# Softmax by a min-reduction, output gates of two pairs together, first gate of the delta rule earlier, 32 products from GpSimd to VectorE

## The chip, the cores and the metric

The kernel runs on one core of a Trainium2 chip. The time is device microseconds of that core; each kernel is run several times and the median counts. TensorE (PE in the profile, PEld for its weight loads) multiplies matrices into PSUM; VectorE (DVE), ScalarE (ACT) and GpSimd (POOL) do everything elementwise; SyncE (SP) issues the DMAs.

## The reference, cut to what matters

The program is a small network on 512 positions of width 1024, all in float32. A first block has two layers of feed-forward, mixer, feed-forward; the mixer of its second layer is a sparse attention ("dsa"). A second block has a gated delta rule ("gdn") and a forgetting attention ("fox"). The change touches these three:

```
# dsa: 8 heads of 128; the keys that are not among the top 256 are masked
s = einsum(q, k_sel) * 128 ** -0.5 ;  p = softmax(where(valid, s, -inf)) ;  o = p @ v

# gdn: 16 value heads, chunks of 128 positions in the kernel
q_dec = q * exp(g)                      # decayed queries
o = q_dec @ state + attn @ v_new        # a scan over the chunks
o = rmsnorm(o, norm_w) * silu(z)        # z: the gate, a projection of the input

# fox: 16 heads of 64
q = rmsnorm(q) * 64 ** -0.5 ; k = rmsnorm(k)          # x * root, per head
logits = q @ k + cum[t] - cum[s], masked causally ; p = softmax(logits) ; o = (p @ v) * silu(z)
```

## The kernel before

Every float32 product is done as three fast matmuls on split operands (a high and a low part: `xh`, `xl` for data, `wh`, `wl` for weights; lines 145 to 147). A weight tile of 128 x 1024 is loaded by SP (`raw`, line 138), cast by ACT to `wh` (139) and subtracted to `wl` by DVE (140); three tiles of each kind rotate. A projection of 128 outputs over the 512 positions is 8 x 3 = 24 matmuls of 512 columns into one PSUM bank of the tag "acc", of which there are three; the bank is free again when its last reader is through.

The kernel is written as one stream of calls. A planner, at build time, draws up the order of each engine's queue: of the instructions that it reckons ready it takes the one that stands first in the stream (`tc.high_priority()` lifts some). So work that stands later fills holes in earlier work, as far as buffers allow, and where a call stands in the stream is its rank. On the chip each engine keeps the drawn-up order and waits where an input is late.

**gdn** (line 967) goes through 8 groups of two value heads. `stage_a(gi)` projects a query and a key tile, convolves them on DVE (1022), normalises them, makes the matrices `Am` and `At` (1121 to 1123), the decayed queries `qd` (1127, on GpSimd, two products of 128 x 512 per group) and the inverse of a triangular system: its small blocks in a chain on DVE (1144, 1146), then DMAs and small matmuls (1169 to 1207). `stage_v` projects and convolves the values, `stage_z` the gate (two projections, a tanh on ACT at 1015 and a product on DVE at 1016, into `zg`, one buffer), `stage_b` is the scan over four chunks, `stage_g` the norm with the gate, `stage_o` the output projection. They are called in the order a(0), a(1), v(0), then for each group v(gi+1), a(gi+2), b(gi), z(gi), g(gi), o(gi-1). `self.late()` (1632) scales the eight tiles of the residual.

**fox** (line 1351) goes through 8 pairs of heads. For pair p there are eight score steps (two heads x four query blocks): `scores` (1466) makes the logits, one DVE instruction adds `ncb` and takes the row maximum (1475), DVE negates it (1477), ACT takes the exponential with its sum (1478), DVE the reciprocal (1479) and the product (1480); `turn` transposes the block (1489, 1490) one step later; `values` (1493) multiplies with v and the gate `zs`. Between these steps, written out by hand, `fill.run` puts in the projections of the next pair, in units of three matmuls: q, k, then for an even pair v, for an odd pair the gates of both pairs (`z_done`, 1432). `normed` squares q or k out of PSUM, makes the root `r` seven units later (173 to 177) and multiplies `x` by it on GpSimd (1403); q and k are then split into halves (1415 to 1425). Exponential and logarithm share one table of ACT, which `self.log_exp()` loads; Silu needs another.

**dsa** (line 784) has the same softmax with the scale as a factor: 895 reduces, 897 multiplies by -DSA_SCALE, 898 exponentiates, 900 multiplies on ACT; 32 steps in all. Beside them runs the top-k of line 881, 882 on DVE.

Of the kernel before, what the change touches and what calls it, by code (L numbers as in the profile page):

```python
# [12 lines left out]
AF = mybir.ActivationFunctionType  # L13
ALU = mybir.AluOpType
# [14 lines left out]
def f32(ap):  # L29
    return ap.bitcast(F32)  # L30
# [410 lines left out]
def c4(ap, c):  # L441
    return ap[:, c * P:(c + 1) * P]
# [275 lines left out]
DSA_SCALE = 128.0 ** -0.5  # L718
TAKEN = -3.0e38
# [64 lines left out]
def dsa(self, tables):  # L784
    nc, tc, A = self.nc, self.tc, self.A
    with tc.tile_pool(name="ds", bufs=1) as ds:
        def T(name, shape=(P, S), dtype=F32, bufs=None):
            return ds.tile(list(shape), dtype, name=name, bufs=bufs)
# [26 lines left out]
        ps = self.bank()  # L815
# [39 lines left out]
        bias = [cneg]  # L855
        for i in range(1, 4):
            W = (i + 1) * P
            x = T(f"isc{i}", (P, W))

            for t in range(2):  # L860
# [3 lines left out]
                for a, ps in enumerate(pair):  # L864
                    hh = 2 * t + a
                    r = self.tmp()
# [22 lines left out]
        def scores(h, i):  # L889
            W = (i + 1) * P  # L890
            ps = self.bank("sa")
            nc.tensor.matmul(ps[:, :W], c4(qT[h], i), kT[h // 4][:, :W], start=True, stop=True)
            x = T("p", bufs=3)[:, :W]
            st = T("st", (P, 4), bufs=4)
            nc.vector.tensor_tensor_reduce(x, ps[:, :W], bias[i], 1.0, TAKEN, op0=ALU.add, op1=ALU.max,
                                           accum_out=st[:, 0:1])
            nc.vector.tensor_scalar(st[:, 1:2], st[:, 0:1], -DSA_SCALE, None, op0=ALU.mult)
            nc.scalar.activation(x, x, AF.Exp, scale=DSA_SCALE, bias=st[:, 1:2], accum_out=st[:, 2:3])
            nc.vector.reciprocal(st[:, 3:4], st[:, 2:3])
            nc.scalar.activation(x, x, AF.Copy, scale=st[:, 3:4])  # L900
            prob[h, i] = x
# [65 lines left out]
def gdn(self, feed0, gate, tail):  # L967
    nc, tc, A = self.nc, self.tc, self.A
    with tc.tile_pool(name="gd", bufs=1) as gd, tc.tile_pool(name="gdd", bufs=1, space=bass.MemoryType.DRAM) as dr:
        def T(name, shape=(P, S), dtype=F32, bufs=None):  # L970
            return gd.tile(list(shape), dtype, name=name, bufs=bufs)
# [10 lines left out]
        ps, ps_q, ps_k = [self.bank() for _ in range(3)]  # L982
# [31 lines left out]
        def silu2(out, x, t):  # L1014
            nc.scalar.activation(t, x, AF.Tanh, scale=0.5)
            nc.vector.scalar_tensor_tensor(out, t, 1.0, x, op0=ALU.add, op1=ALU.mult)
# [55 lines left out]
        def wtile(m):  # L1072
            return self.weights(A["a_in"][m], 1024)

        def stage_a(gi):
# [3 lines left out]
            for u in range(2):  # L1079
                if gi == 0:  # L1080
                    ps = (ps_q, ps_k)[u]
                else:
                    ps = self.bank()
                    self.project(ps, wtile(u * 8 + gi), 0, self.xh, self.xl)
                x = T(f"x{u}", bufs=2 + u)
# [3 lines left out]
            rb, r, pk = norms(qk, 1.0, "sa", gi < 2)  # L1089
# [5 lines left out]
            q, k = qk  # L1095
            kkm, qkm = T("gt", bufs=2), T("gt", bufs=2)
            for src, dst, mi in ((k, kkm, 0), (q, qkm, 1)):
                ps = self.aux()
# [5 lines left out]
            gbc = T("big", (P, 2, S), bufs=3)  # L1104
# [9 lines left out]
            for a in range(2):  # L1114
                e = self.tmp()
                for c in range(4):
                    nc.scalar.activation(c4(e, c), gbc[:, a, c * P:(c + 1) * P], AF.Relu, scale=-1.0,
                                         bias=gcol[:, c, hs[a]:hs[a] + 1])
# [5 lines left out]
            nc.scalar.activation(gbc, gbc, AF.Exp, bias=ln_qs)  # L1124
            qd = T("qd", (P, 2, S), bufs=2)
            for a in range(2):
                nc.gpsimd.tensor_mul(qd[:, a], q, gbc[:, a])

# [35 lines left out]
            for n in range(8):  # L1166
                for q in quart:
                    r = slice(q.start, q.start + 16)
# [42 lines left out]
        def stage_v(gi):  # L1211
            hs = (2 * gi, 2 * gi + 1)
            vn = T("vnat", (P, 4, 2, P), bufs=2)
            for a in range(2):
                ps = self.bank()
                self.project(ps, wtile(16 + hs[a]), 0, self.xh, self.xl)
                x = T("cv", bufs=2)
                conv(ps, 16 + hs[a], x)
                pv = self.bank("sb")
                for c in range(4):  # L1220
                    nc.tensor.transpose(c4(pv, c), c4(x, c), self.ident)
                nc.scalar.activation(vn[:, :, a, :], pv.rearrange("p (c d) -> p c d", c=4), AF.Copy, scale=0.5)
            return vn

        def stage_z(gi):
            zg = T("zg", (P, 2, S))
            for a in range(2):
                ps = self.bank()
                self.project(ps, wtile(32 + 2 * gi + a), 0, self.xh, self.xl)
                silu2(zg[:, a], ps, zg[:, a])  # L1230
            return zg
# [65 lines left out]
        def stage_o(gi, og):  # L1297
            for m4 in range(2):
                wo = self.weights(A["a_out"][gi, m4], 1024)
                for u in range(4):  # L1300
                    m = 4 * m4 + u
                    ps = self.bank()
                    self.project(ps, wo, u * 256, [o[0] for o in og], [o[1] for o in og])
                    with tc.high_priority():
                        nc.vector.scalar_tensor_tensor(self.h[m], ps, gate[:, m:m + 1], self.h[m], op0=ALU.mult,
                                                       op1=ALU.add)

        og, last = {}, []
        st = {gi: stage_a(gi) for gi in range(2)}
        vs = {0: stage_v(0)}  # L1310
        for gi in range(8):
            if gi < 7:
                vs[gi + 1] = stage_v(gi + 1)
            if gi < 6:
                st[gi + 2] = stage_a(gi + 2)
            if gi == 0:
                self.late()
            oT = stage_b(gi, st.pop(gi), vs.pop(gi))
            z = stage_z(gi)
            og[gi] = stage_g(gi, oT, z)  # L1320
            if gi:
                stage_o(gi - 1, og.pop(gi - 1))
# [28 lines left out]
def fox(self, feed, gate, tail):  # L1351
    nc, tc, A = self.nc, self.tc, self.A
    BF = dt.bfloat16
    with tc.tile_pool(name="fx", bufs=1) as fx, tc.tile_pool(name="fxd", bufs=1, space=bass.MemoryType.DRAM) as dr:
        def T(name, shape=(P, S), dtype=F32, bufs=None):
            return fx.tile(list(shape), dtype, name=name, bufs=bufs)
# [13 lines left out]
        ps, ps_q, ps_k = [self.bank() for _ in range(3)]  # L1370
        self.project_halves([(ps, next(feed), 16, 16), (ps_q, next(feed), P, P), (ps_k, next(feed), P, P)])
        fb = self.prm("b_f_bias")[:16]
        e, z, one = self.tmp()[:16], self.tmp()[:16], self.tmp()[:16]
# [13 lines left out]
        qs, ks, vs, zs, og = {}, {}, {}, {}, []  # L1387

        def normed(name, dst, p, gain_col, sq_scale, eps, halves):
            def done(ps):  # L1390
                x, sq, sh = T("x", bufs=2), self.tmp(), T("sqh", dtype=F32R, bufs=2)
                nc.scalar.activation(sq, ps, AF.Square, scale=sq_scale)
                nc.scalar.activation(x, ps, AF.Copy, scale=gain_col)
                nc.scalar.activation(sh, ps, AF.Square, scale=sq_scale)
                sl = T("sql", dtype=F32R, bufs=2)
                nc.vector.tensor_sub(sl, sq, f32(sh))

                def stats():
                    pn = self.bank()
                    nc.tensor.matmul(pn, blk, sh, start=True, stop=False)  # L1400
                    nc.tensor.matmul(pn, blk, sl, start=False, stop=True)
                    r = self.rstd_from(pn, T("r", bufs=2), eps)
                    nc.gpsimd.tensor_mul(x, x, r)  # L1403
                    dst[p] = halves(x)
                fill.later(7, stats)
            return done
# [21 lines left out]
        def v_copy(p):  # L1428
            v = vs[p] = vs[p + 1] = T("v", (P, 4, 256), bufs=2)
            return lambda c2, ps: nc.scalar.copy(v[:, 2 * c2:2 * c2 + 2].rearrange("p c d -> p (c d)"), ps)  # L1430

        def z_done(p):
            def done(ps):
                zs[p] = T("sz", bufs=2)
                nc.scalar.activation(zs[p], ps, AF.Silu)
                self.log_exp()
            return done

        def q_done(p):
# [24 lines left out]
        nbs, prob, pTs = {}, {}, {}  # L1464

        def scores(p, a, i):
            q, (k, kl) = qs[p][:, a], ks[p]
            W = (i + 1) * P
            ps = self.bank("sa")
            nc.tensor.matmul(ps[:, :W], c4(q, i), k[:, a, :W], start=True, stop=False)  # L1470
            nc.tensor.matmul(ps[:, :W], c4(q, i), kl[:, a, :W], start=False, stop=False)
            nc.tensor.matmul(c4(ps, i), ib, mb, start=False, stop=True)
            x = T("p", bufs=3)[:, :W]
            st = T("st", (P, 4), bufs=4)
            nc.vector.tensor_tensor_reduce(x, ps[:, :W], nbs[p][:, a, :W], 1.0, TAKEN, op0=ALU.add, op1=ALU.max,  # L1475
                                           accum_out=st[:, 0:1])
            nc.vector.tensor_scalar(st[:, 1:2], st[:, 0:1], -1.0, None, op0=ALU.mult)
            nc.scalar.activation(x, x, AF.Exp, bias=st[:, 1:2], accum_out=st[:, 2:3])  # L1478
            nc.vector.reciprocal(st[:, 3:4], st[:, 2:3])
            nc.vector.tensor_scalar(x, x, st[:, 3:4], None, op0=ALU.mult)  # L1480
            prob[p, a, i] = x
# [28 lines left out]
        for t in range(len(steps) + 2):  # L1510
            if t < len(steps):
                p, a, i = steps[t]
# [246 lines left out]
```

## Time and profile before

| | |
|---|---|
| runs of the kernel before | 2765.12, 2759.53, 2767.68 us; median 2765.12 |
| the profiled execution | 2762.07 us, its span 2760.3 us, granted clock 0.99 |
| busy, of the span | PE 2674.5 us (97%), PEld 2186.6 (79%), DVE 1719.7 (62%), ACT 1211.2 (44%), POOL 197.4 (7%) |
| stages on the time axis | dsa from about 1280 to 1460 us, gdn from about 1840 to 2400, fox from about 2400 to the end |

PE's busy time is that of pipelined matmuls, one after another without a hole in most of the span; the time that a change can win is where PE waits or runs at the lower clock.

### The profile page before, as it was taken

What the parts mean: (1) busy time and instruction counts of PE and PEld (TensorE: products, weight loads), DVE (VectorE), ACT (ScalarE), POOL (GpSimd) and SP (SyncE); (2) the same over time, 40 slices, a digit from 0 to 9 for tenths busy, and PEclk for the clock granted to TensorE, in tenths of its full rate; (3) what the DMA queues carried; (4) which work ended last, traced back from release to release, by engine and by line L of the source; (5) the groups of instructions that cost most, each with busy time, mean ns of one, the idle gap of its engine ahead of it and who ended that gap; (6) DMA issues with size and microseconds to landing.
All of it is one profiled execution on the core that took longest, in us unless ns stands there. A gap on an engine that the chain in (4) does not pass through costs nothing. (4 is left out here: it accounts for less than half of the span.)

```text
span 2760.3 us, 38266 instructions
## 1 busy us (share of the span) xinstructions
PE 2674.5 (97%) x14903; PEld 2186.6 (79%) x14903; DVE 1719.7 (62%) x3081; ACT 1211.2 (44%) x2248; POOL 197.4 (7%) x184
## 2 busy tenths in 40 slices
PE   8999999999999999999899999999899999999998
PEld 6888878788888888887678888887778777777776
DVE  6454567764545744446966434468788777687776
ACT  4222244532223422223265222246655555577774
POOL 0000002000000000002420000011100000110101
PEclk9999999999999999999999999999999999999999
DMA  5343432244434433333212333223333343132221
GB/s 180 119 138 114 128 97 70 76 140 120 138 114 117 130 112 103 93 94 88 76 39 78 98 99 95 93 76 108 85 115 102 101 113 97 53 101 71 79 65 64
DMA packets 106708, 274.59 MB, mean 99 GB/s; under 512 B 35464, under 2 KB 39552, under 8 KB 106528
## 3 DMA queue, kind: packets, MB, share of 16 engines
q1 hardware_dynamic: 106528, 272.15, 32.6%
q8 instruction: 118, 1.93, 0.3%
q14 instruction: 62, 0.51, 0.1%
HBM read 267.79 MB, written 4.31 MB: 99 GB/s over the span
## 5 line engine op out<-in xcount | busy, mean ns | idle before, releaser
L145 PE MATMUL acc<-xh,wh 128*128 128x512 f32 (+2 forms) x2320 | 909.9, 393 | 21.1 <-ACT xh L186 8.7
L139 ACT CAST wh<-raw 128x1024 fp32r<-128x1024 f32 (+3 forms) x430 | 439.3, 1022 | 1070.0 <-PE acc L146 706.8
L146 PE MATMUL acc<-xl,wh 128*128 128x512 f32 (+1 forms) x2320 | 903.5, 390 | 3.3 <-POOL xl L151 2.4
L147 PE MATMUL acc<-xh,wl 128*128 128x512 f32 (+1 forms) x2320 | 897.8, 387 | 1.8 <-DVE wl L140 1.8
L140 DVE TENSOR_TENSOR wl<-raw,wh 128x1024 fp32r<-128x1024 f32 (+2 forms) x410 | 489.9, 1196 | 80.9 <-ACT wh L139 76.9
L145 PEld LDWEIGHTS acc<-xh,wh 128*128 128x128 f32 (+1 forms) x2320 | 435.9, 188 | 111.8 <-issue 9.1
L146 PEld LDWEIGHTS acc<-xl,wh 128*128 128x128 f32 x2320 | 435.7, 188 | 91.9 <-POOL xl L151 3.9
L147 PEld LDWEIGHTS acc<-xh,wl 128*128 128x128 f32 x2320 | 435.0, 188 | 91.0 <-DVE wl L140 3.2
L146 PE MATMUL acc<-al,wh 128*128 128x512 f32 (+1 forms) x720 | 278.2, 386 | 0.0
L147 PE MATMUL acc<-ah,wl 128*128 128x512 f32 (+1 forms) x720 | 277.7, 386 | 0.0
L145 PE MATMUL acc<-ah,wh 128*128 128x512 f32 (+1 forms) x720 | 277.4, 386 | 0.0
L249 DVE SCALAR_TENSOR_TENSOR h<-acc,h 128x512 f32<-128x512 f32 x128 | 88.4, 690 | 215.8 <-PE acc L147 215.3
L289 DVE TENSOR_TENSOR tmp<-acc,rstd 128x512 f32<-128x512 f32 x88 | 60.9, 691 | 240.3 <-PE acc L147 240.3
L287 DVE TENSOR_TENSOR tmp<-acc,rstd 128x512 f32<-128x512 f32 x88 | 60.8, 691 | 176.7 <-PE acc L147 176.6
L146 PEld LDWEIGHTS acc<-al,wh 128*128 128x128 f32 x720 | 135.2, 188 | 28.7 <-DVE al L151 0.8
L145 PEld LDWEIGHTS acc<-ah,wh 128*128 128x128 f32 x720 | 135.2, 188 | 28.1
L147 PEld LDWEIGHTS acc<-ah,wl 128*128 128x128 f32 x720 | 135.2, 188 | 28.1
L140 POOL TENSOR_TENSOR wl<-raw,wh 128x1024 fp32r<-128x1024 f32 (+1 forms) x20 | 47.8, 2392 | 872.3 <-ACT wh L139 861.2
L145 PE MATMUL acc<-ogh,wh 128*128 128x512 f32 (+1 forms) x256 | 104.0, 408 | 2.4 <-DVE h L310 2.0
L147 PE MATMUL acc<-ogh,wl 128*128 128x512 f32 (+1 forms) x256 | 99.0, 387 | 0.0
L146 PE MATMUL acc<-ogl,wh 128*128 128x512 f32 (+1 forms) x256 | 98.9, 387 | 0.0
L150 ACT CAST ah<-tmp 128x512 fp32r<-128x512 f32 x88 | 54.9, 623 | 63.4 <-DVE tmp L290 63.4
(450 smaller groups left out, 3438.3 us busy)
## 6 DMA issues: line engine op xcount, KB each, us to landing
raw<-in_wi_dram SPq DMA_DIRECT2D x176, 512.0 KB, 3.7
raw<-in_wo_dram SPq DMA_DIRECT2D x64, 512.0 KB, 3.4
raw<-in_ada_w_dram SPq DMA_DIRECT2D x48, 512.0 KB, 3.6
raw<-in_a_in_dram SPq DMA_DIRECT2D x48, 512.0 KB, 3.9
raw<-in_b_in_dram SPq DMA_DIRECT2D x24, 512.0 KB, 3.6
raw<-in_wo_dram SPq DMA_DIRECT2D x24, 384.0 KB, 3.1
raw<-in_a_out_dram SPq DMA_DIRECT2D x16, 512.0 KB, 4.0
big<-rd SPq DMA_DIRECT2D x13, 512.0 KB, 4.9
```

What stands on the lines that cost most here:

```text
L139: nc.scalar.copy(wh[:, :n], raw[:, :n])
L140: self.lo_eng.tensor_tensor(wl[:, :n], raw[:, :n], f32(wh[:, :n]), op=ALU.subtract)
L145: nc.tensor.matmul(out, ah, bh, start=start, stop=False)
L146: nc.tensor.matmul(out, ah, bl, start=False, stop=False)
L147: nc.tensor.matmul(out, al, bh, start=False, stop=stop)
L150: self.nc.scalar.copy(hi, x)
L249: nc.vector.scalar_tensor_tensor(self.h[m], ps, scale(m), self.h[m], op0=ALU.mult, op1=ALU.add)
L287: nc.vector.tensor_mul(t, pg, rstd)
L289: nc.vector.tensor_mul(u, pu, rstd)
```

## The change

In both softmaxes the reduction works on the negated logits and takes their minimum, so that its result is the negated maximum already; the negation goes, and the exponential is taken with scale -1. In gdn the decayed queries, and in fox the products with the root, go from GpSimd to VectorE. In gdn the gate of group 0 is called between a(0) and a(1). In fox the gate of an even pair stays in its PSUM bank until that of the odd pair is there too, and both Silu follow each other, with one reload of the exponential's table behind them.

```diff
@@ dsa scores
-            nc.vector.tensor_tensor_reduce(x, ps[:, :W], bias[i], 1.0, TAKEN, op0=ALU.add, op1=ALU.max,
+            nc.vector.tensor_tensor_reduce(x, ps[:, :W], bias[i], -DSA_SCALE, -TAKEN, op0=ALU.add, op1=ALU.min,
                                            accum_out=st[:, 0:1])
-            nc.vector.tensor_scalar(st[:, 1:2], st[:, 0:1], -DSA_SCALE, None, op0=ALU.mult)
-            nc.scalar.activation(x, x, AF.Exp, scale=DSA_SCALE, bias=st[:, 1:2], accum_out=st[:, 2:3])
+            nc.scalar.activation(x, x, AF.Exp, scale=-1.0, bias=st[:, 0:1], accum_out=st[:, 2:3])
@@ gdn stage_a
             for a in range(2):
-                nc.gpsimd.tensor_mul(qd[:, a], q, gbc[:, a])
+                nc.vector.tensor_mul(qd[:, a], q, gbc[:, a])
@@ gdn, order of the stages
-        st = {gi: stage_a(gi) for gi in range(2)}
+        st = {0: stage_a(0)}
+        z = stage_z(0)
+        st[1] = stage_a(1)
         vs = {0: stage_v(0)}
...
             oT = stage_b(gi, st.pop(gi), vs.pop(gi))
-            z = stage_z(gi)
+            if gi:
+                z = stage_z(gi)
@@ fox normed
-                    nc.gpsimd.tensor_mul(x, x, r)
+                    nc.vector.tensor_mul(x, x, r)
@@ fox z_done
             def done(ps):
-                zs[p] = T("sz", bufs=2)
-                nc.scalar.activation(zs[p], ps, AF.Silu)
-                self.log_exp()
+                zs[p] = ps
+                if p % 2:
+                    for q in (p - 1, p):
+                        ps, zs[q] = zs[q], T("sz", bufs=2)
+                        nc.scalar.activation(zs[q], ps, AF.Silu)
+                    self.log_exp()
@@ fox scores
-            nc.vector.tensor_tensor_reduce(x, ps[:, :W], nbs[p][:, a, :W], 1.0, TAKEN, op0=ALU.add, op1=ALU.max,
+            nc.vector.tensor_tensor_reduce(x, ps[:, :W], nbs[p][:, a, :W], -1.0, -TAKEN, op0=ALU.add, op1=ALU.min,
                                            accum_out=st[:, 0:1])
-            nc.vector.tensor_scalar(st[:, 1:2], st[:, 0:1], -1.0, None, op0=ALU.mult)
-            nc.scalar.activation(x, x, AF.Exp, bias=st[:, 1:2], accum_out=st[:, 2:3])
+            nc.scalar.activation(x, x, AF.Exp, scale=-1.0, bias=st[:, 0:1], accum_out=st[:, 2:3])
```

## Rows read from the trace of the kernel before

**Rows 1.** Windows: span, busy time per engine, PE clock, DMA share, GB/s, by stage.
```profile
core 0: us, PE busy (x) PEld busy (x) DVE busy (x) ACT busy (x) POOL busy (x), PEclk, DMA share, GB/s
...
1320.00:1460.00 140.00, 127.45 (x680) 101.39 (x679) 108.85 (x323) 68.76 (x157) 42.97 (x22) 0.95 0.18 53
...
1880.00:1960.00 80.00, 66.59 (x391) 54.52 (x390) 69.98 (x156) 43.73 (x115) 6.03 (x4) 0.91 0.36 101
1960.00:2400.00 440.00, 433.56 (x3924) 353.16 (x3924) 334.35 (x802) 253.54 (x696) 29.00 (x27) 1.00 0.35 99
...
2460.00:2700.00 240.00, 226.60 (x1276) 179.16 (x1275) 175.08 (x428) 182.34 (x348) 22.34 (x14) 1.00 0.24 74
```

**Rows 2.** PE's timeline at gdn's start: start, length, instruction, idle before, releaser.
```profile
1929.79 0.39 PE L146 MATMUL acc<-xl,wh 128*128 128x512 f32 x1
1930.02 0.39 PE L147 MATMUL acc<-xh,wl 128*128 128x512 f32 x1
1937.85 1.97 PE L1221 MATMUL sb<-ident,cv 128*128 128x128 f32 x8 [7.45 <-DVE cv L1016]
1943.07 0.77 PE L145 MATMUL acc<-xh,wh 128*128 128x512 f32 x1 [3.25 <-DVE cv L1022]
```

**Rows 3.** Windows: the four microseconds behind these two waits.
```profile
1943.00:1947.00 4.00, 3.93 (x10) 3.09 (x11) 4.00 (x8) 0.63 (x1) 0.00 (x0) 0.50 0.16 26
```

**Rows 4.** Groups of instructions, gdn and weights: busy us, mean ns, idle before.
```profile
L140 DVE TENSOR_TENSOR wl<-raw,wh 128x1024 fp32r<-128x1024 f32 (+2 forms) x410 | 489.9, 1196 | 80.9 <-ACT wh L139 76.9 <-DMA big<-ad 3.7
...
L1127 POOL TENSOR_TENSOR qd<-x,big 128x512 f32<-128x512 f32 x16 | 24.9, 1574 | 77.0 <-DVE At L1123 27.8 <-ACT kdec L1241 25.8 <-DVE Am L1121 18.4
...
L1123 DVE TENSOR_TENSOR At<-gt,tmp 128x512 f32<-128x512 f32 x16 | 16.3, 1022 | 2.2 <-PE sb L1265 2.2
...
L1016 DVE SCALAR_TENSOR_TENSOR zg<-zg,acc 128x512 f32<-128x512 f32 x16 | 10.9, 682 | 0.2 <-ACT zg L1015 0.2
...
L1094 DVE TENSOR_TENSOR x<-x,big 128x512 f32<-128x512 f32 x12 | 8.1, 680 | 1.9 <-DMA big<-rd 1.8
```

**Rows 5.** DVE's timeline while GpSimd makes two decayed queries of group 1.
```profile
1932.06 0.68 DVE L1123 TENSOR_TENSOR At<-gt,tmp 128x512 f32<-128x512 f32 x1
...
1933.58 1.63 DVE L1122 TENSOR_TENSOR Am<-Am,gbcol 128x512 f32<-128x512 f32 x1
```

**Rows 6.** GpSimd's timeline in the same stretch.
```profile
1932.81 3.51 POOL L1127 TENSOR_TENSOR qd<-x,big 128x512 f32<-128x512 f32 x2 [27.76 <-DVE At L1123]
```

**Rows 7.** PE's waits in fox and the end: releaser, us in total, times, longest.
```profile
PE sb L1489 <- DVE p L1480: 8.3, 5, 2.2
...
PE sb L1489 <- DVE st L1477: 2.4, 4, 1.6
...
PE sa L1471 <- DVE kl L1425: 2.1, 6, 0.5
```

**Rows 8.** Groups of instructions in fox.
```profile
L1475 DVE CUSTOM_DVE_ANT_0 p<-sa,ncb 128x128 f32<-128x128 f32 (+1 forms) x64 | 31.0, 485 | 9.5 <-PE sa L1472 8.9 <-PE sb L1489 0.5
...
L1403 POOL TENSOR_TENSOR x<-x,r 128x512 f32<-128x512 f32 x16 | 24.9, 1558 | 224.7 <-DVE st L1477 116.3 <-DVE r L177 52.4 <-ACT p L1478 46.1
...
L1435 ACT ACT_TABLE_LOAD x8 | 10.3, 1283 | 0.1
...
L1477 DVE TENSOR_SCALAR st<-st 128x1 f32<-128x1 f32 x64 | 9.5, 148 | 0.8
```

**Rows 9.** DVE's timeline ahead of one of PE's waits of 2.2 us.
```profile
2578.65 1.37 DVE L1480 TENSOR_SCALAR p<-p,st 128x384 f32<-128x384 f32 x1
...
2583.33 0.69 DVE L1475 CUSTOM_DVE_ANT_0 p<-sa,ncb 128x512 f32<-128x512 f32 x1
...
2583.94 1.22 DVE L140 TENSOR_TENSOR wl<-raw,wh 128x1024 fp32r<-128x1024 f32 x1
2585.08 0.15 DVE L1477 TENSOR_SCALAR st<-st 128x1 f32<-128x1 f32 x1
```

**Rows 10.** PE's longest wait in dsa.
```profile
PE sa L892 <- DVE st L895: 9.3, 2, 7.1
```

## The prediction

> **What bounds the kernel now.** I read the busy line of the page first: PE is busy 97% of the span, the next engine 62%. So what another engine saves counts only where PE stands waiting for it. The windows by stage show where that is. Over most of the span PE has no hole; it has them in dsa's top-k stretch (12.6 of 140 us idle), in the first 80 us of gdn (13.4 idle, clock 0.91), and in fox's pair loop (13.4 of 240) [rows 1]. The rest of gdn has 6.4 us idle in 440, so it is full [rows 1]. The list of PE's waits then gives names. In gdn's start there are two long ones, 7.45 and 3.25 us, both for DVE's convolution of a value tile, which has to free one of the three "acc" banks or be transposed [rows 2]; right behind them the granted clock is 0.50, the lower level of 1.2 GHz, for 4 us [rows 3]. In fox the waits are short and come back at each pair: 8.3 + 2.4 + 2.1 = 12.8 us for the normalised probabilities, the negated maximum and the low half of k [rows 7]. In dsa it is one wait for the reduction, whose engine is in the top-k [rows 10].
>
> **gdn, the gate of group 0.** Nothing is added to the total; two projections change rank. One projection is 24 matmuls that start 0.23 us apart [rows 2], two are 48 x 0.23 = 11.0 us of PE. With them go two weight loads on SP's queue, which now stand ahead of the four of a(1) and v(0) and take two turns of the three rotating tiles; two casts and two tanh on ACT, which is busy 44 of 80 us there [rows 1]; and on DVE two subtractions of 1.20 and two products of 0.68, 3.8 us [rows 4]. A gate's bank is free after one tanh and one DVE product of 0.68 us, whereas a query's or value's needs three convolution steps; so PE gets 11.0 us of work that hardly leans on the engine that holds it up. DVE is what limits this start (70 of 80 us [rows 1]), so its 3.8 us push the convolutions back by as much. The holes to be filled are 7.45 + 3.25 us, and behind them 4 us at half rate, which cost 2 us: 12.7 together. I count 11.0 - 3.8 - 0.7 (next part) = 6.5, and take 6. The ends are 12.7 (all gone) and, on the other side, the second rival. What is late next: the scan of group 0 used these 11 us as filler, and now has to draw on v(2) and a(3), for which two value buffers and three banks are there; `zg` has one buffer, so z(1) cannot come forward.
>
> **gdn, decayed queries on DVE.** 16 products of 1.57 us leave POOL [rows 4]; on DVE each costs what the like-shaped product of x does, 0.68, 10.9 us over 440 in which DVE is busy 334 [rows 1, 4]. Something comes back. While POOL works, DVE's products stretch: 1.63 us in place of 0.68 in the 3.51 us of two POOL products [rows 5, 6], and the At product, which is often beside them, takes 1.02 on average, 16 x 0.34 = 5.4 us over the stage [rows 4]. Net +5 us of DVE at most, under a PE that is full: 0 in the steady part. In the start four of the products fall in (2.7 us), and about 2 come back: +0.7. If the cover were gone, the price would be the 5 us; the gain's end is 0.
>
> The Trainium skill ("GPSIMD Engine Reference", 8. Key points) says that GpSimd shares its SBUF interfaces with VectorE, which clashes with VectorE instructions in a two-port mode or with two SBUF inputs. The rows agree, and in fox they show it for an instruction with one tensor input too: the product of 128 x 384 took 1.37 us [rows 9]. The sum would be the same by either.
>
> **fox, root product on DVE.** 16 x 0.68 = 10.9 us come to DVE, and 64 negations of 0.148, 9.5 us, go [rows 4, 8]: its load stays at about 175 of 240 [rows 1]. What counts is the chain from the root to the next pair's first scores: root, product, casts, low halves, logits, transposes. The product in it takes 1.56 us on POOL [rows 8] and 0.68 on DVE: 0.88 less, for q and for k. What stands behind it on DVE (a probability product, a reduction) waits 0.68 longer but is no longer stretched.
>
> **Both softmaxes, no negation.** In the chain the negation is 0.15 us, but also a second place in DVE's queue: in the stretch ahead of a wait of 2.2 us, the reduction ends at 2583.9, a weight subtraction of 1.22 slips in, and the negation is through at 2585.2 [rows 9]. Without it the exponential can start about 1.2 us earlier, if ACT is free; ACT has a weight cast there, so I count a half. Whether a minimum with a factor costs what the maximum does, the trace doesn't show: the same form took 0.485 us on average [rows 8], and that is what I take; the worst would be a second pass, 64 x 0.485 = 31 us on DVE in fox, and of a gain there is no sign.
>
> **fox, gates together.** Four of eight loads of Silu's table go, and with each one load back: 8 x 1.28 = 10.3 us of ACT's 182 [rows 1, 8]. The load that goes stood in the middle of the odd pair, between the root and the casts of k; the block that stays is longer by one Silu. By itself I cost it at 0, since PE's waits name DVE; its price if a bank runs short is the first rival.
>
> For fox together: 0.88 + 0.6 + 0.15 = 1.6 us off a chain that makes PE wait 12.8 / 7 = 1.8 us per pair [rows 7]. Not all of these waits hang on it, and the planner will draw up another order; I take 1.0 us x 7 = 7. The ends are 0 and 12.8.
>
> **dsa.** 32 negations of about 0.15 (the like of rows 8) are 4.7 us, of which a third falls where DVE is full. The long wait [rows 10] is for the top-k and stays. I take 1; the ends are 0 and 4.7.
>
> **Sum.** 6 + 0 + 7 + 1 = 14 us. The profiled execution took 2762.07 (span 2760.3 and 1.8 around it), so 2748; it lies 3.05 under the median of the runs, which gives 2751.
>
> **Rivals.** *A bank runs short in fox (chance 0.10).* The gate of the even pair holds a bank through the odd one's projection and until Silu has read it; of three banks one is left for the roots' sums and the next query. For it: the bank comes free only behind a table load and a Silu, about 1.9 us, plus what ACT has ahead. Against it: the root of k is long done by then. If PE waits there, it is 4 times 1.9 to 3 us, 8 to 12, and eats fox's gain: 2751 + 7 + 5 = 2763. The Trainium skill ("Perfetto Trace Analysis", Optimization Strategy) says that the same gap coming back on the engine that should be saturated can mean too little PSUM or SBUF; by it fox's repeated waits would be such gaps and would grow here. The rows name DVE's results as releasers, not a bank [rows 7], so I give it no more than a tenth.
>
> *The early gate only shifts the hole (0.10, the slower side).* If DVE stays the limit up to the scan of group 0, PE's two waits remain, and behind them the scan and the second group's triangular chain find no filler: PE, which was full there, loses up to the 11.0 us that it had. That decides if v(2) and a(3) cannot be drawn forward. Then gdn costs 11 + 3.8 instead of gaining 6: 2751 + 6 + 15 = 2772, with DVE's 5 us of gdn up to 2777.
>
> *The gate's move is worth nothing (0.15).* The planner fills the same holes otherwise, and the later stretch loses what the start wins: 2757.
>
> *More goes than I count (0.15).* All of the 12.7 and 12.8 us and 3 in dsa: 2765 - 28.5 = 2737.
>
> **How the numbers follow.** The forecast has 0.50, with 2743 to 2758 of its own. A measurement of this kernel tells 0.3%, 8.3 us, from no change: faster is under 2756.8, slower over 2773.4. Faster: 0.47 of the forecast, 0.15 and 0.06 of the third, 0.68, taken down to 0.66 for the order that I can't see; slower: 0.06 of the second rival and 0.03 of unknowns (a dearer reduction), 0.09; same 0.25. The range leaves out the outer part of the second and fourth case: 2737 to 2768.
>
> **What would show it.** Right: in gdn's first 100 us PE's two waits shrink to under 5 us together and the 0.50 stretch is gone, with the rest of gdn still full; DVE's At product is back at 0.68; in fox the waits for probabilities fall under 7 us, ACT shows four Silu table loads, and the reduction with the minimum keeps 0.485. Wrong: new PE waits with ACT's Silu or a bank as releaser at the end of odd pairs, or PE idle behind the first scan; above all if gdn's end does not come earlier against its start.

## The result, and the profile after

The changed kernel takes 2731.8 us in the median of 4 runs (2728.1 to 2734.0) against 2765.0 (2759.5 to 2767.7) of the kernel before: ratio 0.9881, 95% interval 0.9862 to 0.9900. It gains 33 us where 14 were forecast. The sign was right, the size was not: the time lies below the range.

The busy line of the page after: PE 97% before, 98% now, and GpSimd at 148 us.

```profile
PE 2662.3 (98%) x14903; PEld 2186.1 (80%) x14903; DVE 1708.8 (63%) x3017; ACT 1207.0 (44%) x2246; POOL 147.9 (5%) x152
```

One instruction marks the stages: L310 writes the residual at a stage's tail. From its first `h<-acc,h` to its first `h<-acc,mod,h` is gdn, from there to its last is fox. Before, then after (duration min/median/max, first and last start):

```profile
L310 DVE SCALAR_TENSOR_TENSOR h<-acc,mod,h x32: 471/476/485, 2397.6 to 2747.0; 128x256 f32<-128x256 f32 x32
L310 DVE SCALAR_TENSOR_TENSOR h<-acc,h x16: 407/414/425, 1836.4 to 1857.6; 128x256 f32<-128x256 f32 x16
```

```profile
L310 DVE SCALAR_TENSOR_TENSOR h<-acc,mod,h x32: 470/476/485, 2382.0 to 2713.0; 128x256 f32<-128x256 f32 x32
L310 DVE SCALAR_TENSOR_TENSOR h<-acc,h x16: 406/414/425, 1830.8 to 1851.9; 128x256 f32<-128x256 f32 x16
```

So up to gdn 1836.4 became 1830.8, gdn 561.2 became 551.2, and fox 349.4 became 331.0: 5.6 + 10.0 + 18.4 = 34.0, all of the difference of the spans.

The windows after that answer to [rows 1] (columns as there):

```profile
core 0: us, PE busy (x) PEld busy (x) DVE busy (x) ACT busy (x) POOL busy (x), PEclk, DMA share, GB/s
1320.00:1460.00 140.00, 127.14 (x688) 103.80 (x687) 104.43 (x291) 68.13 (x155) 41.03 (x22) 0.96 0.17 53
1880.00:1960.00 80.00, 77.79 (x509) 64.01 (x509) 75.56 (x185) 44.97 (x119) 0.00 (x0) 0.98 0.44 121
1960.00:2370.00 410.00, 401.18 (x3701) 329.37 (x3702) 312.68 (x747) 240.55 (x670) 9.37 (x13) 1.00 0.34 100
...
2430.00:2690.00 260.00, 259.43 (x1477) 209.96 (x1475) 193.13 (x432) 199.07 (x383) 0.00 (x0) 1.00 0.24 79
```

The start of gdn is nearly full (2.2 us idle of 80, before 13.4) and its clock is 0.98. In fox's pair loop 0.6 us of idle time is left of 260. dsa's top-k stretch is as it was (12.9 idle of 140). PE's waits agree. Between 2450 and 2700 us one line is all that is left for [rows 7] (releaser, us in total, times, longest):

```profile
PE acc L145 <- ACT xh L150: 0.2, 1, 0.2
```

Over the whole run, the top-k wait of dsa [rows 10] now stands at the transposes, and four short waits in gdn stand for [rows 2]:

```profile
PE sb L907 <- ACT p L900: 8.2, 1, 8.2
...
PE sb L1221 <- DVE cv L1016: 3.7, 4, 1.1
```

The groups after, for [rows 4] and [rows 8] (busy, mean ns, idle before): the At product is back at 0.68 us, both moved products cost 0.68 to 0.69 on VectorE, and the reduction with the minimum costs what the maximum did.

```profile
L1483 DVE CUSTOM_DVE_ANT_0 p<-sa,ncb 128x128 f32<-128x128 f32 (+1 forms) x64 | 30.9, 483 | 10.0 <-PE sa L1479 9.8
...
L1406 DVE TENSOR_TENSOR x<-x,r 128x512 f32<-128x512 f32 x16 | 11.0, 688 | 0.2
```

```profile
L1123 DVE TENSOR_TENSOR At<-gt,tmp 128x512 f32<-128x512 f32 x16 | 10.7, 683 | 0.0
L1127 DVE TENSOR_TENSOR qd<-x,big 128x512 f32<-128x512 f32 x16 | 10.6, 680 | 0.0
```

One thing that the diff seems to say did not happen: Silu's table is still loaded for each of the eight gates, and fox has 18 loads of tables in all where it had 20. ScalarE's timeline at the end of an odd pair (start, length) shows why. The even pair's gate (2460.39) waits for nothing once its bank is full, so it is issued as early as it can be; an exponential follows it and needs the other table again, and the odd pair's gate brings two more.

```profile
2459.09 1.28 ACT L1442 ACT_TABLE_LOAD   x1
2460.39 0.60 ACT L1442 ACTIVATE sz<-acc 128x512 f32<-128x512 f32 x1
2460.88 0.26 ACT L1497 COPY pT<-sb 128x128 f32<-128x128 f32 x1
2461.16 1.28 ACT L1485 ACT_TABLE_LOAD   x1
2462.45 0.62 ACT L1485 ACTIVATE p<-p,st 128x384 f32<-128x384 f32 x1
...
2466.73 1.28 ACT L1442 ACT_TABLE_LOAD   x1
2468.02 0.60 ACT L1442 ACTIVATE sz<-acc 128x512 f32<-128x512 f32 x1
2468.64 1.28 ACT L126 ACT_TABLE_LOAD   x1
```

### The profile page after: what moved, and what is told of

Read it like the earlier page. It is cut to its first block, busy times and chain, and to the rows that moved or that the text cites. A ratio compares the mean times of both kernels' runs of the same rounds, so it can differ in the third digit from the quotient of the medians.

```text
span 2726.3 us, 38166 instructions
## 1 busy us (share of the span) xinstructions
PE 2662.3 (98%) x14903; PEld 2186.1 (80%) x14903; DVE 1708.8 (63%) x3017; ACT 1207.0 (44%) x2246; POOL 147.9 (5%) x152
```

## Where the list of waits was short

Fox did the same work before and after, 1914 matmuls and as much weight-load time, yet PE's "busy" fell by 5.2 us along with the idle time. Whole stages, gdn then fox, before and after:

```profile
1836.40:2397.60 561.20, 534.32 (x4545) 438.45 (x4545) 439.70 (x1018) 329.92 (x880) 53.59 (x56) 0.98 0.34 97
2397.60:2747.00 349.40, 327.25 (x1914) 264.12 (x1912) 256.22 (x593) 248.14 (x481) 43.73 (x44) 1.00 0.22 70
```

```profile
1830.80:2382.00 551.20, 532.35 (x4545) 439.94 (x4544) 440.36 (x1034) 328.75 (x880) 28.66 (x40) 0.99 0.34 99
2382.00:2713.00 331.00, 322.08 (x1914) 263.83 (x1912) 248.89 (x544) 244.97 (x479) 18.85 (x28) 0.99 0.23 74
```

Idle time by the view is 349.4 - 327.25 = 22.15 us before and 331.0 - 322.08 = 8.92 after, 13.2 less; the stage became 18.4 shorter. The rest sat under the modelled ends of the matmuls. The pair loop alone, from the first to the last start of the values' matmuls (`mg<-pT,v`), shows it with the clock at 1.00 before and after: it became 17.6 us shorter, and only 13.1 of them had been called idle.

```profile
2488.00:2731.90 243.90, 230.84 (x1295) 182.07 (x1294) 172.11 (x412) 168.93 (x327) 19.75 (x12) 1.00 0.22 70
```

```profile
2471.60:2697.90 226.30, 226.30 (x1294) 181.57 (x1294) 164.11 (x368) 167.00 (x325) 0.00 (x0) 1.00 0.23 75
```

PE's timeline before at one hole:

```profile
2584.98 0.28 PE L1470 MATMUL sa<-ks,qs 128*128 128x256 f32 x1
2585.10 0.28 PE L1471 MATMUL sa<-kl,qs 128*128 128x256 f32 x1
2587.54 0.63 PE L1489 MATMUL sb<-ident,p 128*128 128x128 f32 x4 [2.16 <-DVE p L1480]
```

The starts are 2.44 us apart and 2.16 are called idle, although such a matmul is followed by the next after 0.12 us where nothing holds it (2584.98 to 2585.10). The Trainium skill ("Perfetto Trace Analysis", Tensor Engine Instruction (MATMUL, LD_WEIGHTS)) says that the profiler computes a matmul's end from its size, and another section (Identifying the Most-Contended Engine) reads the weight-load share instead. The trace agrees: weight loads took 264.1 and 263.8 us. That share was in [rows 1]: 179.16 / 240 = 0.747 in the pair loop, against 353.16 / 440 = 0.803 in full gdn. 240 x (1 - 0.747 / 0.803) = 16.7 us of holes, where the busy column gave 13.4 and the list 12.8. The loop after, which has no idle time, checks this measure: its share is 181.57 / 226.3 = 0.802, and by it the loop before held 243.9 - 182.07 / 0.802 = 16.9 us of holes, where 17.6 went.

## The experiments

The stages follow one another, so each run's gdn and fox are read by L310 as above, and fox's pair loop by the values' matmuls. "All" is the changed kernel; lengths are from one profiled execution each. With gdn as in "all", 11 profiles gave 550.7 to 554.2 us, mean 551.9; with fox as in "all", 7 gave 331.0 to 331.7, mean 331.3. The loop repeats best: with its code as in "all", 8 profiles gave 226.2 to 226.3 us, while the stretch of fox ahead of it took 88.6 to 92.5 over all the runs. So a part of fox that is worth a few us is read from the loop.

| run | base and edit | gdn us | fox us | its loop us | median us | ratio to before, 95% |
|---|---|---|---|---|---|---|
| before | | 561.2 | 349.4 | 243.9 | 2765.0 | |
| all | before + the change | 551.2 | 331.0 | 226.3 | 2731.8 | 0.9862 to 0.9900 |
| p1 | before + no dsa negation, early gate, gates together | 557.5 | 351.1 | 244.8 | 2757.2 | 0.9964 to 0.9984 |
| p2 | before + both products on VectorE | 557.7 | 334.5 | 229.0 | 2743.4 | 0.9913 to 0.9942 |
| p3 | before + no fox negation | 562.9 | 349.2 | 241.6 | 2762.9 | 0.9987 to 1.0006 |
| w1 | all, fox negation back | 552.5 | 333.9 | 228.0 | 2736.3 | 0.9879 to 0.9912 |
| w2 | all, root product back on GpSimd | 551.0 | 343.3 | 235.9 | 2745.3 | 0.9921 to 0.9951 |
| w3 | all, gates apart | 552.0 | 332.1 | 226.2 | 2731.6 | 0.9878 to 0.9907 |
| w4 | all, decayed queries back on GpSimd | 554.7 | 331.7 | 226.2 | 2735.8 | 0.9888 to 0.9923 |
| w5 | all, gate late | 556.7 | 331.0 | 226.3 | 2738.3 | 0.9898 to 0.9927 |
| x3 | all, root later on VectorE | 551.5 | 335.6 | 230.8 | 2736.7 | 0.9887 to 0.9920 |
| x1 | all + idle GpSimd beside the root product | 552.5 | 335.8 | 230.0 | 2737.6 | 0.9893 to 0.9922 |
| x1b | all + idle GpSimd off the chain | 552.4 | 332.5 | 226.8 | 2735.5 | 0.9884 to 0.9913 |
| x4 | all + x3 + x1 | 551.2 | 341.2 | 234.2 | 2742.6 | 0.9915 to 0.9948 |
| x5 | all + idle GpSimd in gdn | 568.4 | 331.1 | 226.3 | 2745.7 | 0.9924 to 0.9958 |
| x2 | all, the two gates adjacent | 554.2 | 331.6 | 226.0 | 2735.1 | 0.9883 to 0.9913 |
| y1 | all, rotary adds on VectorE | 550.7 | 331.7 | 226.2 | 2731.6 | 0.9879 to 0.9906 |
| y2 | y1 + dsa's weight subtractions on VectorE | 551.4 | 331.1 | 226.3 | 2739.2 | 0.9905 to 0.9932 |
| z1 | all, gdn memsets on VectorE | 549.1 | 331.3 | 226.2 | 2730.5 | 0.9858 to 0.9891 |
| z2 | all, input splits on VectorE | 550.1 | 329.9 | 226.2 | 2729.8 | 0.9861 to 0.9891 |

**One part alone.** p1 takes three parts of the change's diff, one in each stage; p2 the two products; p3 fox's softmax.

```diff
# p2
-                nc.gpsimd.tensor_mul(qd[:, a], q, gbc[:, a])
+                nc.vector.tensor_mul(qd[:, a], q, gbc[:, a])
...
-                    nc.gpsimd.tensor_mul(x, x, r)
+                    nc.vector.tensor_mul(x, x, r)
```

> The kernel before with three parts of the change, one in each stage: no negation in dsa, group 0's gate early in gdn, gates grouped in fox. Its stages do not overlap, so each is read by its own length (before: gdn 561.2 us, fox 349.4; after: 551.2 and 331.0). My theory now: gdn's 10 us are the early gate's, which fills two PE holes; fox's 18 are the root product's; the grouping is worth nothing, since the trace after still has 16 table loads in fox. So gdn 551 to 553, fox 348 to 350, total near 2765 - 2 - 9 = 2754. Rival 1, gdn gains because GpSimd no longer slows VectorE (decayed queries): gdn stays at 559 to 562, total 2763. Rival 2, fox gains from the grouping: fox 332 to 340, total near 2742.

> The kernel before with the decayed queries (gdn) and the root products (fox) on VectorE, nothing else. Theory A, the root product's path: fox 332 to 337 us (before 349.4), gdn unchanged at 560 to 562, total near 2765 - 14 = 2751. Theory B, the negation's place in VectorE's queue: fox 345 to 349, total 2762. Rival for gdn (the decayed queries' contention with VectorE): gdn 551 to 555 instead.

> The kernel before without the negation in fox, nothing else. Theory A (root product's path): fox 344 to 349 us, total 2760 to 2765. Theory B (a place in VectorE's queue, 64 times): fox 332 to 338, total near 2750. If each of the two parts alone brings most of the gain, because PE is then full and can give no more, both this and the kernel with the root products on VectorE show fox under 338.

p2 settles what carries most of fox: the root products alone bring 14.9 us, in the stage and in the loop, and PE's waits in the pair loop go with them. p3 brings 0.2 of the stage but 2.3 of the loop, since its start of fox was 2.1 us longer than before; the gates in p1 cost 1.7 and 0.9. For gdn my expectation missed twice: the gate alone gives 557.5, not 551 to 553, and the queries, forecast at 0, give 557.7.

**All but one part.** w1 to w5 each undo one part (the lines are those of the change's diff, taken back).

> The kernel after, with the negation in fox put back. Theory A (root product's path): fox 331 to 335 us, total 2732 to 2736. Theory B (the negation): fox 343 to 349, total 2744 to 2750. A full PE (either part is enough): 331 to 333, total 2732 to 2734.

> The kernel after, with the root products of fox back on GpSimd. Theory A (root product's path): fox 343 to 349 us (after 331.0), total 2744 to 2750. Theory B (the negation): fox 331 to 335, total 2732 to 2736.

> The kernel after, with the gates of fox apart again. The grouping changes nothing, since both kernels load tables 16 times in fox: 331 us for fox, total 2731 to 2733. Rival, the later first gate takes ScalarE out of the middle of the odd pair: fox 334 to 340, total 2735 to 2741. Rival, the grouping holds a bank and costs: fox 328 to 330, total 2729.

> The kernel after, with gdn's decayed queries back on GpSimd. If gdn's gain is the early gate's: gdn 551 to 552 us (after 551.2), total 2732 to 2733. If part of it is VectorE left alone by GpSimd: gdn 554 to 559, total 2735 to 2740.

> The kernel after, with group 0's gate of gdn back behind its scan. If gdn's gain is the early gate's: gdn 559 to 561 us, total 2740 to 2742. If it is the decayed queries': gdn 551 to 553, total 2732 to 2734. Half and half: 555 to 557.

w2 gives back 12.0 us (9.6 of the loop), and PE's waits of [rows 7] are there again between 2450 and 2700 us. w1 gives back 2.6 (1.7 of the loop), as theory A said, and w3 0.8 (nothing of the loop). The parts of fox do not simply add: w2's loop is still 8.0 us shorter than before, where p3 shows 2.3 for the negation and p1 a loss for the gates. What makes up the rest is not shown; another order drawn up by the planner is one candidate.

```profile
PE sb L1493 <- DVE p L1484: 5.3, 9, 1.3
PE sa L1476 <- DVE kl L1427: 2.0, 6, 0.4
```

In gdn the four combinations now stand: neither part 562.0 (before and p3), gate only 556.1 (p1 and w4), queries only 557.2 (p2 and w5), both 551.9. So the gate is worth 5.9 or 5.3, the queries 4.8 or 4.2, and they add: both are about half, as w5's third case had it. Why the queries cost is not shown by w4: the orders of VectorE's and PE's instructions in its gdn are others than the changed kernel's, so the planner is a rival there beside contention.

**Late, or slowed?** GpSimd's root product is 0.9 us longer than VectorE's, and it also slows VectorE's work beside it. x3 makes only the first, x1 only the second, x4 both; x1b starts x1's work earlier, ahead of the root, off that part of the chain.

```diff
# x3 (and x4)
                     r = self.rstd_from(pn, T("r", bufs=2), eps)
+                    nc.vector.tensor_scalar(r, r, 2.0, None, op0=ALU.mult)
+                    nc.vector.tensor_scalar(r, r, 0.5, None, op0=ALU.mult)
# x1 (and x4)
+                    for u in range(2):
+                        nc.gpsimd.tensor_mul(T("hq", (P, 256), bufs=4), r[:, u * 256:u * 256 + 256], r[:, 0:256])
                     nc.vector.tensor_mul(x, x, r)
```

> The kernel after, with the root of fox doubled and halved again on VectorE before its product: two more instructions of 128x512, about 0.4 us each, so that the product comes 0.8 to 0.9 us later, as it did on GpSimd (1.6 against 0.69 us), with nothing on GpSimd. Theory L (fox's 15 us are the length of the chain from root to scores): fox 341 to 346 us (after 331.0), total near 2743. Theory C (contention: GpSimd's product slows what VectorE does beside it): fox 331 to 334, total 2732 to 2735.

> The kernel after, with a product on GpSimd beside each of VectorE's root products in fox whose result nobody reads (two of 128x256, about 0.8 us each, started when the root is there). Theory L (length of the chain): fox 331 to 335 us, unless VectorE's own product is itself slowed. Theory C (contention beside the chain): fox 340 to 346, VectorE's root product at 1.1 to 1.5 us in place of 0.69.

> The kernel after, with the same two idle products on GpSimd, started earlier, when the low part of the squares is there, some 7 units of the projections before the root: as much GpSimd time, but beside whatever VectorE does then. Theory L: fox 331 to 333 us. Theory C in any place: fox 336 to 344. If GpSimd hurts only where VectorE works for the chain, this stays at 331 to 334 while the run with the products beside the root goes up.

> The kernel after, with both at once in fox: the root doubled and halved again on VectorE (the product 0.85 us later) and, beside the product, the idle products on GpSimd. Alone they gave fox 335.6 and 335.8 us (after 331.0). If these two make up what the root products on GpSimd cost, and add: 340 to 341 us; with the product on GpSimd itself it was 343.3. If they are one and the same delay seen twice: 336 to 338.

Neither theory alone: in the loop, lateness costs 230.8 - 226.3 = 4.5 us, idle work beside the product 3.7, both 7.9 (of the stage 4.3, 4.5 and 9.9). They add, and make up 7.9 of the 9.6 that w2 gives back there. Off the chain the idle work costs 0.5 (1.2 of the stage). VectorE's and ScalarE's instructions stand in the same order in x1's and x1b's loops as in the changed kernel's, and nothing in x1 waits for the idle products, so what x1 costs is VectorE being slowed. The place is not the only difference to x1b, though: VectorE's busy time in the loop rises from 164.11 by 8.1 us in x1 and by 4.7 in x1b (x1, then x1b).

```profile
2480.10:2710.10 230.00, 228.17 (x1294) 181.25 (x1294) 172.19 (x367) 166.36 (x323) 27.03 (x24) 1.00 0.25 74
```

```profile
2479.90:2706.70 226.80, 226.80 (x1295) 181.50 (x1294) 168.80 (x368) 166.94 (x325) 18.90 (x24) 1.00 0.25 75
```

In x1, VectorE's product takes 853 ns in place of 688, and GpSimd's own halves 1131 (in x1b 854):

```profile
L1408 DVE TENSOR_TENSOR x<-x,r 128x512 f32<-128x512 f32 x16 | 13.7, 853 | 0.2
```

```profile
L1407 POOL TENSOR_TENSOR hq<-r 128x256 f32<-128x256 f32 x32 | 35.6, 1131 | 202.7 <-DVE r L177 175.6 <-DVE st L1488 27.1
```

x3 is not purely lateness: its two instructions, 0.42 us each, also take VectorE's time, and the planner's order in the loop is another. Its waits in the pair loop list only 0.6 us, so most of its 4.5 us is again under modelled ends: PE's "busy" in the loop rises from 226.30 to 229.88 for the same 1294 matmuls, with the clock at 1.00.

```profile
2477.10:2707.90 230.80, 229.88 (x1294) 183.02 (x1294) 171.15 (x392) 166.85 (x325) 0.00 (x0) 1.00 0.24 74
```

**Idle work in gdn.** x5 puts two products of 128x256 beside each decayed query.

```diff
                 nc.vector.tensor_mul(qd[:, a], q, gbc[:, a])
+                for u in range(2):
+                    nc.gpsimd.tensor_mul(T("junk", (P, 256)), q[:, u * 256:u * 256 + 256], gbc[:, a, 0:256])
```

> The kernel after, with idle products on GpSimd in gdn (four of 128x256 for each group of heads) that start with the decayed queries on VectorE and whose result nobody reads. If the decayed queries' 4 to 5 us are contention with VectorE: gdn 555 to 557 us (other runs with both changes 551 to 552.5), total 2736 to 2738. If they are the queries' own lateness: gdn 551 to 553.

A miss: gdn grows by 16.5 us. VectorE's busy time rises from 440.4 to 452.7, and PE's "busy" by 8.3 for the same 4545 matmuls.

```profile
1832.70:2401.10 568.40, 540.67 (x4545) 443.77 (x4545) 452.71 (x1034) 328.78 (x880) 61.66 (x72) 0.98 0.33 96
```

```profile
L1123 DVE TENSOR_TENSOR At<-gt,tmp 128x512 f32<-128x512 f32 x16 | 14.9, 945 | 0.0
L1127 DVE TENSOR_TENSOR qd<-x,big 128x512 f32<-128x512 f32 x16 | 14.6, 926 | 0.0
```

A part of the 16.5 us is the clock's. Behind a wait of PE for VectorE, the granted clock is 0.50, the lower level of 1.2 GHz, for 13 us in which PE is busy throughout; by this row some 6.5 us are lost there, an estimate, and most of the rise of PE's "busy" is that. The changed kernel has no such stretch in this place.

```profile
2037.14 0.69 PE L1191 MATMUL mg<-tcp,Am 32*32 32x32 f32 x32 [1.93 <-DVE tcp L1163]
```

```profile
2039.00:2052.00 13.00, 13.00 (x97) 9.77 (x97) 5.33 (x13) 5.23 (x19) 0.52 (x1) 0.50 0.15 40
```

GpSimd beside VectorE can thus cost more than the 4 to 5 us of the queries; VectorE's order in gdn is the changed kernel's. That contention is the whole of the queries' price is not shown: the idle products last 33.2 us against the queries' 24.9 [rows 4], hold the query and decay buffers for longer, and stand ahead of a memset in GpSimd's queue (one wait of 1.3 us is put down to that).

**Gates truly together.** x2 holds the two in program order.

```diff
-                        nc.scalar.activation(zs[q], ps, AF.Silu)
+                        self.tc.keep_in_program_order(nc.scalar.activation(zs[q], ps, AF.Silu))
```

> The kernel after, with the two Silus of a pair of gates in fox held in program order, so that they really stand next to each other: 4 loads of Silu's table and 4 back in place of 16. The load time that goes, 8 x 1.28 = 10.3 us of ScalarE, is off the path, since PE has no holes left in fox's loop: fox 330 to 332 us, total 2731 to 2733. Rival, ScalarE's loads do hold up probabilities: fox 322 to 328. Rival, a bank held for longer costs PE: fox 334 to 342.

Now fox has 10 loads in place of 18, and stays at 331.6 (226.0 in the loop): those 10.3 us of ScalarE were off the path.

```profile
L126 ACT ACT_TABLE_LOAD x6 | 7.7, 1283 | 0.1
L1442 ACT ACT_TABLE_LOAD x4 | 5.1, 1283 | 0.1
```

**GpSimd's other work.** y1, y2, z1 and z2 change `gpsimd` to `vector` in one kind of line each: the rotary adds, these and dsa's weight subtractions, two memsets of gdn, the split of every second input tile.

> The kernel after, with the adds of the rotary embedding in dsa (12 on GpSimd, 1.29 us each and beside a VectorE that is 97% busy from 1320 to 1380 us) on VectorE. If GpSimd's work costs VectorE as much as it would take there: the stretch up to gdn 1829 to 1831.5 us, total 2730 to 2732. If it is worth more to have GpSimd idle: PE's idle time of 8.5 us in 1320 to 1380 shrinks by 2 to 5, total 2727 to 2730. If VectorE is the bound there: 2733 to 2738.

> The kernel after, with the rotary adds and dsa's 20 weight subtractions (2.39 us each on GpSimd, 1.19 on VectorE, 47.7 us in all) on VectorE, so that dsa has next to nothing on GpSimd. VectorE gets up to 24 us more of work in 1275 to 1435 us, where it is 60 to 97% busy. If VectorE is the bound in 1320 to 1380: dsa 4 to 10 us longer, total 2736 to 2742. If contention cost it as much: total 2727 to 2732.

> The kernel after, with the two memsets of each group of gdn (12 us of GpSimd in all: 8 of 0.96 us, 8 of 0.52 us) on VectorE. If any GpSimd work in gdn's loop costs by contention as the decayed queries did (4.5 us for 23.6 us of GpSimd): gdn 549 to 550 us (after 551.2, others up to 552.5), total 2729 to 2730. If memsets, which read nothing, do not disturb VectorE: gdn 551 to 553, total 2731 to 2733.

> The kernel after, with the 16 subtractions of GpSimd at the starts of gdn and fox (0.85 us each) on VectorE, which is 85% busy there. PE's waits with them as releaser are 2.1 us. If VectorE frees more than it takes on: total 2727 to 2730. If VectorE is the bound at both starts, as for dsa's additions (y2): 2732 to 2738.

y1 changes nothing that can be told. y2 loses: gdn begins at 1840.8 us, against 1830.8 to 1836.9 in the other runs, so where VectorE is the bound GpSimd's help is worth its price. z1 and z2 have medians 1 to 2 us under the changed kernel's, in the direction of contention, but the intervals overlap: they are not shown to beat it.

## Why the prediction was wrong, step by step

- **The gate of group 0: 6.** Measured 5.3 to 5.9. Mechanism and size hold: both long waits of [rows 2] and the stretch at 0.50 behind them are gone. The clock's share was read too small: it stood at 0.50 up to 1948, not for 4 us, and PE was busy for 6.8 us at that level, so about 3.4 us were lost and not 2. A little comes back as the second rival had it, four waits of 3.7 us together. The stretch before, then the same stretch after:

```profile
1938.00:1948.00 10.00, 6.75 (x22) 5.32 (x23) 9.77 (x19) 3.16 (x6) 0.00 (x0) 0.50 0.15 40
```

```profile
1930.00:1950.00 20.00, 20.00 (x99) 16.58 (x98) 19.82 (x49) 11.86 (x24) 0.00 (x0) 1.00 0.45 121
```

- **Decayed queries: 0. Failed.** They are worth 4.2 to 4.8. I summed VectorE's time, found it under a full PE, and called it covered. In w4 the At product takes 1.14 us again. x5 makes a price from contention plausible, and does not separate it from the queries' buffers and queue or from the planner's order. The cause stays open.
- **Fox: 7. This is the step that failed most**, in the words "1.6 us off a chain that makes PE wait 12.8 / 7 = 1.8 us per pair. [...] I take 1.0 us x 7 = 7. The ends are 0 and 12.8." Measured 18.1 (17.6 in the loop). First, the upper end was too low. The values' first matmuls, two pairs apart, show it (PE's timeline before, then after): 68.3 us became 62.7, 2.8 per pair, while the list showed 1.8.

```profile
2522.62 1.08 PE L1498 MATMUL mg<-pT,v 128*64 128x512 f32 x4
...
2590.95 1.40 PE L1498 MATMUL mg<-pT,v 128*64 128x512 f32 x6
```

```profile
2503.12 1.08 PE L1505 MATMUL mg<-pT,v 128*64 128x512 f32 x4
...
2565.81 1.40 PE L1505 MATMUL mg<-pT,v 128*64 128x512 f32 x6
```

  Second, of those 1.8 I took half, and all of it went. Third, the product's share counted only its length; x1 shows nearly as much again from VectorE being slowed next to the chain (3.7 us against x3's 4.5), which the prediction named ("no longer stretched") and gave no size.
- **No negation in fox: 0.75 of the 1.6 per pair.** In the loop it brings 2.3 us alone and 1.7 on top of the rest, some 0.3 per pair: less than half of what I gave it. (The stage lengths, 0.2 and 2.6, carry the scatter of fox's start.)
- **Gates together: "Four of eight loads of Silu's table go."** None of the eight went. It cost the forecast nothing, since I had priced ScalarE's time at 0, and x2 shows that this price was right.
- **dsa: 1.** Gdn begins at 1835.3 us on average in the three profiles with the negation and at 1834.5 in the fifteen without it whose dsa is otherwise the same; with a scatter of 6 us that fits 1, and shows no more.
- **The sum.** 0.8 + 10.1 + 18.1 = 29.0 us is what the stages carry over all runs. The other 5 of the 34 between the two profiles lie ahead of gdn, where the changed kernel's was early (1830.8) and others with the same code there came as late as 1836.9. In the runs taken beside the experiments the kernel before had medians of 2760.9 to 2763.9 us, so a few of the 33 are scatter, and that the time fell as far as it did below the range is in part luck; the miss in fox is not.
- **The rivals.** No bank ran short: no wait on one is in fox's pair loop, and the rule of the Trainium skill ("Perfetto Trace Analysis", Optimization Strategy) that I had set beside this rival (repeated gaps as a lack of PSUM) did not apply. "More goes than I count" came nearest: its sum, 28.5 us, is close to the 29.0, but not by its terms. It had 12.8 for fox, the whole list of waits, where 18.1 went, 12.7 for the start of gdn and 3 for dsa, where 10.1 and 0.8 went.

## What to carry to other kernels

Size PE's holes by its weight-load share, or start to start, against a full stretch of the same kernel; the list of waits gives their places and too little of their length. When an operation leaves GpSimd, count its length on the chain and, separately, what it did to VectorE next to that chain; where VectorE itself is the bound, as in dsa in y2, leave it there. Regrouping instructions in the source is not regrouping on the engine: look in the timeline whether another instruction still stands between them.

## What was not expected of the hardware

The same idle GpSimd work cost fox's loop 3.7 us beside the root product and 0.5 us elsewhere, where it slowed VectorE about half as much. The slowing goes both ways: GpSimd's half products take 1131 ns in x1 and 854 in x1b. An instruction with one tensor input is slowed too, the probability product from 385 to 413 ns on average in x1.
